# Background modulation units in a two-layer hybrid transformer block: from three engines to VectorE, TensorE and layer 1

## The chip, the cores and the metric

The kernel runs on one core of a Trainium2 chip, as one program. The core has TensorE (PE in the profile; PEld is its weight load), VectorE (DVE), ScalarE (ACT) and GpSimd (POOL); SyncE (SP) issues most DMA transfers. Each engine works through its own queue in order. The metric is device time in microseconds (us) from one launch.

## The reference

Two residual layers run over 512 tokens (`x`) of width 2048, with 256 context tokens beside them. Layer 0 mixes a pooling branch with latent attention, layer 1 a bidirectional mLSTM with windowed attention. What the change touches is the modulation ahead of and behind each layer:

```python
sc = silu(c); scc = silu(c_ctx)                       # two vectors of 2048
for i in range(2):
    shift, scale, gate       = split(sc  @ ada_w[i] + ada_b[i], 3)
    shift_c, scale_c, gate_c = split(scc @ ada_w[i] + ada_b[i], 3)
    h  = rmsnorm(x,  norm_w[i]) * (1 + scale)   + shift
    hc = rmsnorm(xc, norm_w[i]) * (1 + scale_c) + shift_c
    y, yc = mix_i(h, hc)
    x  = x  + gate   * y
    xc = xc + gate_c * yc          # layer 0 only
return rmsnorm(x, final_norm)
```

`ada_w[i]` is a 2048 x 6144 fp32 matrix: two thin vector-matrix products for each layer, of which most of the cost is reading the matrix. The context's gate of layer 1 is not needed.

## The kernel before

**Matmuls.** Activations lie with channels on partitions, as 16 chunks of 128 channels by tokens. Each large fp32 product is made of three fp32r matmuls, of high and low halves of weight and activation. `load_w` (line 111) loads 512 KB of weights by SP's queue into one of three buffers `wraw`, and `split` (line 107) makes the halves: `wh` by a cast on ScalarE (L108), `wl` by a subtraction on VectorE (L109), four buffers each. One such load feeds a quarter of a group: 4 chunks of the contraction by 256 output channels. `tmode` (L289 for the tokens, `px`, 512 columns; L291 for the context, `pc`, 256 columns) and `kmode` (L302) issue the matmuls.

**Modulation units.** The 12,288 modulation columns are cut into 24 units of 512 columns: 0 to 7 shift and scale of layer 0, 8 to 11 its gates, 12 to 19 shift and scale of layer 1, 20 to 23 its gates. A unit reads 4 MB. Units below 20 need two vectors (tokens and context), the four last ones only one. There are two ways to compute a unit:

- `ada_steps` (line 134), used for units 0 to 7 at the start: TensorE multiplies 16 tiles `at` of 128 x 512 fp32 by the columns of `st` (the two vectors, padded to 32 columns), four tiles at a time in four strips of 32 output partitions of one PSUM tile `pa` (L143). VectorE transposes `pa`, and a small matmul `pb` (L150) folds the partial sums.
- `ada_vec_steps` (line 154), used for units 8 to 23 in the background: for each of 16 tiles `at`, VectorE multiplies by the first vector and adds into `acc0` (L162 for the first tile, L164 after that); for two-vector units ScalarE multiplies the same tile by the second vector in place (L167), and GpSimd adds it into `acc1` (L169). Each tile is one step. One more step for each accumulator transposes it (L174) and reduces it (L175). The unit's `pb` matmul (L181) and four small additions (`ada_place`, L131) come 16 steps into the next unit.

`Background` (line 186) strings such units into one sequence of steps, of which other code asks for a number at a time.

**Order of the work.** At the start TensorE's order is written by hand: units 1 to 7 among the first in-projection groups. Behind that the in-projection of layer 0 runs in `in_group` calls for groups 2 to 13 (line 484), four quarters each, with two background steps before and two after each quarter's matmuls: 192 steps are asked for, and units 8 to 17 have 180. Groups 2 and 3 make the query's latent, whose statistics (`cps`, L247) follow; groups 4 to 7 the pooling branch, with `pool_mean` and `pool_mix` between the quarters of 5 and 7; groups 8 to 13 the attention gates. Then comes attention (TensorE's order by hand again), then the out-projection of layer 0, whose function `out0` (line 883) asks for four background steps a quarter: units 18 to 23, 104 steps. Layer 1 begins with `h_chunk` and its in-projection. `mv_group` (line 1164) makes the mLSTM values for three heads, while the gate arithmetic of the mLSTM runs in the pool `gs` on VectorE and ends; `ctx_state` follows each; then group 5. No background runs in layer 1. The layer 1 gates (units 20 to 23) are first used at the very end, in `out_evac`.

Where no order is written by hand, a planner in the compiler lays out each engine's queue from its own estimates of durations, in the program's order as far as operands and buffers are ready. A tile's buffer is given again only when its last reader is done; the queue that asks for it waits. Background tiles have four buffers (`nb`, tag `ada`), shared by all units of the sequence.

Of the kernel before, what the change touches and what calls it, by code (L numbers as in the profile page):

```python
# [8 lines left out]
F32 = mybir.dt.float32  # L9
F32R = mybir.dt.float32r  # L10
AF = mybir.ActivationFunctionType
ALU = mybir.AluOpType
# [4 lines left out]
P = 128  # L17
# [21 lines left out]
def tile_hybrid_dit(ctx: ExitStack, tc: tile.TileContext, ts: dict, out: bass.AP, dbg=None, upto=99):  # L39
# [94 lines left out]
    def ada_steps(u, pp, tp, nb=3, nt=2):  # L134

        pa = pp.tile([P, 512], F32, name=f"pa{u}", tag="pm")
        for q in range(4):
# [13 lines left out]
                ada_place(u, pb, 2)  # L151
            yield

    def ada_vec_steps(u, pp, tp, nb, ttag, tbufs):

        both = u < 20
        acc = [tp.tile([P, 512], F32, name=f"acc{u}_{v}", tag=f"acc{v}", bufs=1) for v in range(2 if both else 1)]
        for kc in range(16):
            at = tp.tile([P, 512], F32, name=f"at{u}_{kc}", tag="ada", bufs=nb)
            DM.dma_start(at, ts["ada"][u, kc // 2][:, (kc % 2) * 512 : (kc % 2) * 512 + 512])  # L160
            if kc == 0:
                V.tensor_scalar(acc[0], at, st[:, kc, 0:1], None, op0=ALU.mult)  # L162
            else:
                V.scalar_tensor_tensor(acc[0], at, st[:, kc, 0:1], acc[0], op0=ALU.mult, op1=ALU.add)  # L164
            if both:
                m = acc[1] if kc == 0 else at
                S.mul(m, at, st[:, kc, 1:2])  # L167
                if kc:
                    G.tensor_tensor(acc[1], acc[1], m, op=ALU.add)  # L169
            yield  # L170
        red = tiny.tile([P, 2, 16], F32, name="red", tag="red", bufs=2)
        for v in range(len(acc)):
            tr = tp.tile([P, 512], F32, name="atr", tag=ttag, bufs=tbufs)
            V.transpose(tr, acc[v])  # L174
            V.tensor_reduce(red[:, v, :], tr.rearrange("p (b r) -> p b r", r=32), axis=AX.X, op=ALU.add)  # L175
            yield

        def finish():
            n = len(acc)
            pb = pp.tile([32, 2, 16], F32, name=f"pb{u}", tag="pm")  # L180
            T.matmul(pb[:, :n, :], fold, red[:, :n, :], start=True, stop=True)  # L181
            ada_place(u, pb, n)

        return finish
# [108 lines left out]
    def kmode(ps, w, kcs, Hs, first, last, share):  # L293

        for i, kc in enumerate(kcs):
            wh, wl = w[i]
            for b, p_ in enumerate(ps):
                Hh, Hl = Hs[kc][0][:, b * P : (b + 1) * P], Hs[kc][1][:, b * P : (b + 1) * P]
                for n, (h_, w_) in enumerate(((Hh, wh), (Hh, wl), (Hl, wh))):
                    s0 = first and i == 0 and n == 0 and b % share == 0  # L300
                    s1 = last and i == len(kcs) - 1 and n == 2
                    T.matmul(p_, h_, w_, start=s0, stop=s1, skip_group_check=True)  # L302
# [96 lines left out]
    with tc.manual_schedule(engines={mybir.EngineType.PE}):  # L399
        ht = Ring(sp, 2)  # L400
# [38 lines left out]
    def ta(name, n=NT):  # L439
        return ap_.tile([P, NP], F32, name=name, tag="ta", bufs=6)[:, :n]  # L440
# [38 lines left out]
    S.copy(kr[:, NX:], pc[:, 0, :])  # L479
    split(kr, KH, KL)  # L480

    bg = Background(range(8, 18), pp, ap_, 4, "ta", 6)

    def in_group(g, between=()):
        px, pc = new_px(2), new_pc()
        for kq in range(4):
            w = load_w(win[g, kq])
            bg.step(2)
            tmode(px, [pc[:, b, :] for b in range(2)], w, range(4 * kq, 4 * kq + 4), HX0, HC0, kq == 0, kq == 3)
            bg.step(2)  # L490
            if kq < len(between):
                between[kq]()
        return px, pc
# [1 line left out]

    ssq = [ap_.tile([P, NT], F32, name="ssqc", tag="ssqc", bufs=1), 0]
    for g in range(2):
        px, pc = in_group(2 + g)
        for b, r in enumerate(c_evac([(px[b], pc[:, b, :]) for b in range(2)], ssq)):
            G.dma_start(cqd[2 * g + b], r)  # L500
    p6 = pp.tile([P, 6], F32, name="cps6", tag="pm")
# [45 lines left out]
        return z  # L547

    for pr in range(2):
        px, pc = in_group(4 + 2 * pr)  # L550
        ds, zs = [], []

        def mean(b):
            ds.append(pool_mean(2 * pr + b, px[b], pc[:, b, :]))

        def mix(b):
            zs.append(pool_mix(2 * pr + b, ds[b]))

        mean(0)
        qx, qc = in_group(5 + 2 * pr, (lambda: mean(1), lambda: mix(0), lambda: None, lambda: mix(1)))  # L560
        for b in range(2):
            t = ta("psg")
            S.activation(t[:, :NX], qx[b], AF.Silu)
            S.activation(t[:, NX:], qc[:, b, :], AF.Silu)
            V.tensor_tensor(t, zs[b], t, op=ALU.mult)
            G.dma_start(zd[2 * pr + b], t)


    for i in range(6):
        px, pc = in_group(8 + i)  # L570
        for b in range(2):
            t = ta("sag")
            S.activation(t[:, :NX], px[b], AF.Silu)
            S.activation(t[:, NX:], pc[:, b, :], AF.Silu)
            G.dma_start(agd[2 * i + b], t)
# [302 lines left out]
    esP.close()  # L878
    esP = ExitStack()
    pp = ppool(esP, "ppO", px=4, pc=2, pm=2)  # L880
    bg = Background(range(18, 24), pp, tz, 4, "ht", 3)

    def out0(g, vs, between=None):
        px = new_px(2) if 0 in vs else None
        pc = new_pc() if 1 in vs else None
        for kq in range(4):
            w = load_w(ts["ev_out"][g, kq])
            if g == 1 and kq < 3:
                zc_load(kq + 1)
            bg.step(4)  # L890
            tmode(px, pc and [pc[:, b, :] for b in range(2)], w, range(4 * kq, 4 * kq + 4), ZX, ZC, kq == 0, kq == 3)
            next(between, None) if between else None
        out0_evac(g, vs, px, pc)

    def stats1(v):

        nb = (4, 2)[v]
        p6 = pp.tile([P, 6], F32, name="ps6b", tag="pm")
        stat_mm(p6[:, :nb], ssq1[v], nb, D)
        rows(rstd_col(p6[:, :nb], nb), nb, pp, ssq1[v])  # L900
# [8 lines left out]
    ehx, ehc, eht = (ExitStack() for _ in range(3))  # L909
    hxp = opool(ehx, "hx", side="right")  # L910
    HX = [(hxp.tile([P, NX], F32R, name=f"hxh{j}"), hxp.tile([P, NX], F32R, name=f"hxl{j}")) for j in range(KC)]
    stats1(0)

    def hx_chunks():
# [7 lines left out]
        out0(g, (1,), hxs)  # L922
    for _ in hxs:
        pass
    bg.finish()
    etz.close()
    ezc.close()

# [232 lines left out]
    eg.close()  # L1161


    def mv_group(h):
        px, pc = new_px(2), new_pc()
        pv = [px[b // 2][:, 256 * (b % 2) : 256 * (b % 2) + 256] for b in range(4)]
        for kq in range(4):
            w = load_w(odw[1 + h, kq])
            kcs = range(4 * kq, 4 * kq + 4)
            kmode(pv, w, kcs, HX, kq == 0, kq == 3, 2)  # L1170
            kmode([pc[:, b, :] for b in range(2)], w, kcs, HC, kq == 0, kq == 3, 2)
        vx_store(h, [p_.rearrange("p (a b) -> p a b", b=256) for p_ in px])
        return vc_store([pc])
# [20 lines left out]
    px, pc = new_px(2), new_pc()  # L1194
    for kq in range(4):
        w = load_w(odw[5, kq])
        tmode(px, [pc[:, b, :] for b in range(2)], w, range(4 * kq, 4 * kq + 4), HX, HC, kq == 0, kq == 3)
    for b in range(2):
        t = cm.tile([P, NX], F32, name="akx", tag="kxt", bufs=2)
        S.copy(t, px[b])  # L1200
        G.dma_start(akd[b][:, :NX], t)
# [630 lines left out]
```

## Time and profile before

| | |
|---|---|
| median of 3 runs | 2345.47 us (2341.54 to 2346.82) |
| profiled execution | 2345.14 us, its span 2343.4 us |
| mean granted TensorE clock | 0.985 |
| TensorE busy | 2238.1 us of the span |
| VectorE, ScalarE, GpSimd busy | 1488.9, 1041.4, 459.0 us |
| background accumulation on VectorE (L164) | 240 instructions, 250.3 us |
| background multiplication on ScalarE (L167) | 180 instructions, 130.0 us |
| background addition on GpSimd (L169) | 180 instructions, 282.7 us |

Rough stages by start in us: start-up and first groups to 180; in-projection groups to 618; attention to 1040; out-projection to 1320; the layer 1 projections, the mLSTM, the windowed attention and the last out-projection to 2343. In a page's rows by line, the two numbers behind the bar are busy time in us and mean duration in ns, and after the second bar stands how long the engine was idle just before them and what ended it. In rows of waits: who waited for whom, us in total, times, longest.

### The profile page before, as it was taken

What the parts mean: (1) busy time and instruction counts of PE and PEld (TensorE: products, weight loads), DVE (VectorE), ACT (ScalarE), POOL (GpSimd) and SP (SyncE); (2) the same over time, 40 slices, a digit from 0 to 9 for tenths busy, and PEclk for the clock granted to TensorE, in tenths of its full rate; (3) what the DMA queues carried; (4) which work ended last, traced back from release to release, by engine and by line L of the source; (5) the groups of instructions that cost most, each with busy time, mean ns of one, the idle gap of its engine ahead of it and who ended that gap; (6) DMA issues with size and microseconds to landing.
All of it is one profiled execution on the core that took longest, in us unless ns stands there. A gap on an engine that the chain in (4) does not pass through costs nothing.

```text
span 2343.4 us, 34744 instructions
## 1 busy us (share of the span) xinstructions
PE 2238.1 (96%) x12920; PEld 1902.8 (81%) x12920; DVE 1488.9 (64%) x2748; ACT 1041.4 (44%) x2054; POOL 459.0 (20%) x393
## 2 busy tenths in 40 slices
PE   5999998999999999999999999999999999999997
PEld 3678887778889999877888898998888877777886
DVE  5578888875476666777767722522555576778435
ACT  4234454443244444554224522222655557666433
POOL 0015565764200000026212200000000010003111
PEclk9999999999999999999999999999999999999998
DMA  9854554563311111255775322123233212113434
GB/s 383 323 197 161 171 185 140 202 205 123 99 57 48 59 52 64 91 186 198 241 248 178 116 95 82 64 73 114 99 99 97 99 62 72 64 55 126 135 113 140
DMA packets 118586, 311.27 MB, mean 133 GB/s; under 512 B 13676, under 2 KB 21356, under 8 KB 118416
## 3 DMA queue, kind: packets, MB, share of 16 engines
q1 hardware_dynamic: 111536, 281.73, 35.9%
q0 software_dynamic: 6880, 27.32, 3.0%
q8 instruction: 101, 1.65, 0.3%
q14 instruction: 69, 0.57, 0.1%
HBM read 279.37 MB, written 29.62 MB: 132 GB/s over the span
## 4 chain that ended last, share of the span: by engine, by line
PE 68%; DVE 9%; issue 4%; DMA 3%; POOL 2%; ACT 2%; DVEq 0%; SPq 0%; ACTq 0%; POOLq 0%
PE px L289 20%; PE px L302 11%; PE pj L619 5%; PE pc L291 5%; PE px L1418 5%; PE s L682 4%; PE pc L302 3%; PE om L725 3%; PE pj L639 2%; POOL acc L169 2%; DMA at<-in_ada_dram 2%; PE s L1418 2%; DVE acc L164 2%; PE po L1337 2%; DVE wl L109 2%
## 5 line engine op out<-in xcount | busy, mean ns | idle before, releaser
L109 DVE TENSOR_TENSOR wl<-wraw,wh 128x512 fp32r<-128x512 f32 (+2 forms) x556 | 431.9, 783 | 420.3 <-ACT wh L108 417.1
L108 ACT CAST wh<-wraw 128x512 fp32r<-128x512 f32 (+2 forms) x556 | 324.5, 589 | 594.7 <-PE pc L291 145.9
L169 POOL TENSOR_TENSOR acc<-acc,at 128x512 f32<-128x512 f32 x180 | 282.7, 1571 | 282.7 <-ACT at L167 272.9
L164 DVE SCALAR_TENSOR_TENSOR acc<-at,st,acc 128x512 f32<-128x512 f32 x240 | 250.3, 1043 | 52.1 <-DMA at<-in_ada_dram 48.3
L167 ACT ACTIVATE at<-at,st 128x512 f32<-128x512 f32 x180 | 130.0, 724 | 180.2 <-DVE acc L164 152.8
L302 PE MATMUL px<-wh,hxh 128*128 128x512 f32 (+2 forms) x512 | 174.4, 341 | 0.1
L302 PE MATMUL px<-wl,hxh 128*128 128x512 f32 (+2 forms) x512 | 173.7, 339 | 0.0
L302 PE MATMUL px<-wh,hxl 128*128 128x512 f32 (+2 forms) x512 | 173.6, 339 | 0.0
L289 PE MATMUL px<-h0h,wl 128*128 128x512 f32 x384 | 155.3, 404 | 11.7 <-DVE wl L109 11.7
L289 PE MATMUL px<-h0h,wh 128*128 128x512 f32 x384 | 156.0, 406 | 1.0 <-ACT wh L108 0.8
L289 PE MATMUL px<-h0l,wh 128*128 128x512 f32 x384 | 153.7, 400 | 0.0
L291 PE MATMUL pc<-h0h,wl 128*128 128x256 f32 x400 | 113.9, 285 | 0.0
L291 PE MATMUL pc<-h0h,wh 128*128 128x256 f32 x400 | 113.7, 284 | 0.0
L291 PE MATMUL pc<-h0l,wh 128*128 128x256 f32 x400 | 113.6, 284 | 0.0
L302 PEld LDWEIGHTS px<-wh,hxh 128*128 128x128 f32 x512 | 96.2, 188 | 12.8 <-ACT sz L1261 1.0
L302 PEld LDWEIGHTS px<-wl,hxh 128*128 128x128 f32 x512 | 96.3, 188 | 11.3
L302 PEld LDWEIGHTS px<-wh,hxl 128*128 128x128 f32 x512 | 96.2, 188 | 11.0
L289 PEld LDWEIGHTS px<-h0h,wl 128*128 128x128 f32 x384 | 73.5, 191 | 32.2 <-DVE wl L109 15.5
L289 PE MATMUL px<-zxh,wl 128*128 128x512 f32 x224 | 88.9, 397 | 3.6 <-DVE wl L109 3.6
L289 PE MATMUL px<-zxh,wh 128*128 128x512 f32 x224 | 89.6, 400 | 2.0 <-ACT wh L108 1.1
L289 PEld LDWEIGHTS px<-h0h,wh 128*128 128x128 f32 x384 | 73.9, 193 | 19.5 <-ACT wh L108 2.5
L289 PE MATMUL px<-hxl,wh 128*128 128x512 f32 x224 | 89.2, 398 | 0.0
(877 smaller groups left out, 6231.7 us busy)
## 6 DMA issues: line engine op xcount, KB each, us to landing
at<-in_ada_dram SPq DMA_DIRECT2D x256, 256.0 KB, 3.1
at<-in_ada_dram SPq DMA_DIRECT2D x64, 512.0 KB, 8.2
wraw<-in_od_in_dram SPq DMA_DIRECT2D x64, 512.0 KB, 3.5
wraw<-in_ev_in_dram SPq DMA_DIRECT2D x56, 512.0 KB, 4.1
wraw<-in_ev_out_dram SPq DMA_DIRECT2D x44, 512.0 KB, 4.5
wraw<-in_od_out_dram SPq DMA_DIRECT2D x36, 512.0 KB, 3.5
wraw<-in_od_oz_dram SPq DMA_DIRECT2D x32, 512.0 KB, 3.5
xt<-in_xT_dram SPq DMA_DIRECT2D x16, 384.0 KB, 7.5
```

Of the source, the lines that this page charges most:

```text
L108: S.copy(h, src)
L109: low.tensor_tensor(l, src, h, op=ALU.subtract)
L164: V.scalar_tensor_tensor(acc[0], at, st[:, kc, 0:1], acc[0], op0=ALU.mult, op1=ALU.add)
L167: S.mul(m, at, st[:, kc, 1:2])
L169: G.tensor_tensor(acc[1], acc[1], m, op=ALU.add)
L289: T.matmul(px[b], w_, Hx[kc][r_], start=s0, stop=s1)
L291: T.matmul(pc[b], w_, Hc[kc][r_], start=s0 and b == 0, stop=s1, skip_group_check=True)
L302: T.matmul(p_, h_, w_, start=s0, stop=s1, skip_group_check=True)
L619: T.matmul(t, w_, r_[:, sl], start=kc == 0 and n == 0, stop=kc == 3 and n == 2)
L682: T.matmul(s[:, c0 - k0 : c1 - k0], l_, r_[:, c0:c1], start=n == 0, stop=n == 4)
L725: T.matmul(o[:, :256], v_[:, 6 - nk + b, :], p_[:, b, :], start=b == 0 and n == 0, stop=b == nk - 1 and n == 2)
L1418: T.matmul(px[b], w_, Hs[kc][r_], start=first and i == 0 and n == 0, stop=last and i == len(kcs) - 1 and n == 2)
```

## The change

Background units no longer use ScalarE (but for the first tile of the second vector) or GpSimd: VectorE accumulates both vectors, so a two-vector step has two accumulations on VectorE. The 16 background units are placed anew:

- units 8 to 13 stay in the in-projection, with two steps before and two after a quarter in groups 2, 3 and 10 to 13, one before a quarter in groups 4 and 6, and none in 5, 7, 8 and 9: 104 steps are asked for, 108 are there, and `bg.finish()` behind group 13 runs the rest;
- units 18 and 19 go to TensorE under groups 8 and 9, by a new function `ada_pe_steps`, which is `ada_steps` with 16 tiles of 256 KB in the four `ada` buffers in place of 8 of 512 KB; one group of four matmuls follows each quarter;
- units 14 to 17, all with two vectors, go to the out-projection of layer 0, three steps a quarter (72 steps), to be finished before layer 1's statistics;
- units 20 to 23, with one vector, go to layer 1: two steps before and three amid each quarter of `mv_group`, two before each quarter of group 5 (68 steps), in a new pool `ada1`, opened when the gate arithmetic's pool is closed.

```diff
+    def ada_pe_steps(u, pp, tp, nb):
+        pa = pp.tile([P, 512], F32, name=f"pa{u}", tag="pm")
+        for q in range(4):
+            at = []
+            for i in range(4):
+                kc = 4 * q + i
+                at.append(tp.tile([P, 512], F32, name=f"at{u}_{kc}", tag="ada", bufs=nb))
+                DM.dma_start(at[i], ts["ada"][u, kc // 2][:, (kc % 2) * 512 : (kc % 2) * 512 + 512])
+            for qd in range(4):
+                T.matmul(pa[32 * qd : 32 * qd + 32, :], st[:, 4 * q + qd, :], at[qd], start=q == 0, stop=q == 3, skip_group_check=True)
+            if q == 3:
+                tr = ta("gat", 512).rearrange("p (b r) -> p b r", r=32)
+                V.transpose(tr.rearrange("p b r -> p (b r)"), pa)
+                yield
+                pb = pp.tile([32, 2, 16], F32, name=f"pb{u}", tag="pm")
+                T.matmul(pb, fold, tr[:, :, 0:2].rearrange("p b v -> p v b"), start=True, stop=True)
+                ada_place(u, pb, 2)
+            yield
...
             if kc == 0:
                 V.tensor_scalar(acc[0], at, st[:, kc, 0:1], None, op0=ALU.mult)
+                if both:
+                    S.mul(acc[1], at, st[:, kc, 1:2])
             else:
-                V.scalar_tensor_tensor(acc[0], at, st[:, kc, 0:1], acc[0], op0=ALU.mult, op1=ALU.add)
-            if both:
-                m = acc[1] if kc == 0 else at
-                S.mul(m, at, st[:, kc, 1:2])
-                if kc:
-                    G.tensor_tensor(acc[1], acc[1], m, op=ALU.add)
+                for v, a in enumerate(acc):
+                    V.scalar_tensor_tensor(a, at, st[:, kc, v : v + 1], a, op0=ALU.mult, op1=ALU.add)
...
-    bg = Background(range(8, 18), pp, ap_, 4, "ta", 6)
+    bg = Background(range(8, 14), pp, ap_, 4, "ta", 6)
-    def in_group(g, between=()):
+    def in_group(g, between=(), steps=(1, 1)):
...
-            bg.step(2)
+            bg.step(steps[0])
             tmode(px, [pc[:, b, :] for b in range(2)], w, range(4 * kq, 4 * kq + 4), HX0, HC0, kq == 0, kq == 3)
-            bg.step(2)
+            bg.step(steps[1])
...
-        px, pc = in_group(2 + g)
+        px, pc = in_group(2 + g, steps=(2, 2))
...
-        px, pc = in_group(4 + 2 * pr)
+        px, pc = in_group(4 + 2 * pr, steps=(1, 0))
...
-        qx, qc = in_group(5 + 2 * pr, (lambda: mean(1), lambda: mix(0), lambda: None, lambda: mix(1)))
+        qx, qc = in_group(5 + 2 * pr, (lambda: mean(1), lambda: mix(0), lambda: None, lambda: mix(1)), (0, 0))
...
-        px, pc = in_group(8 + i)
+        if i < 2:
+            pe = ada_pe_steps(18 + i, pp, ap_, 4)
+            px, pc = in_group(8 + i, (lambda: next(pe), lambda: next(pe), lambda: next(pe), lambda: (next(pe), next(pe))), (0, 0))
+        else:
+            px, pc = in_group(8 + i, steps=(2, 2))
...
-    bg = Background(range(18, 24), pp, tz, 4, "ht", 3)
+    bg = Background(range(14, 18), pp, tz, 4, "ht", 3)
...
-            bg.step(4)
+            bg.step(3)
...
+    bg.finish()
     stats1(0)
...
-    bg.finish()
     etz.close()
...
+    ea = ExitStack()
+    bg = Background(range(20, 24), pp, opool(ea, "ada1"), 4, "atr", 1)
     def mv_group(h):
...
+            bg.step(2)
             kmode(pv, w, kcs, HX, kq == 0, kq == 3, 2)
+            bg.step(3)
             kmode([pc[:, b, :] for b in range(2)], w, kcs, HC, kq == 0, kq == 3, 2)
...
+        bg.step(2)
         tmode(px, [pc[:, b, :] for b in range(2)], w, range(4 * kq, 4 * kq + 4), HX, HC, kq == 0, kq == 3)
+    bg.finish()
+    ea.close()
```

## Prediction

> **What bounds the kernel now.** I read the page first, then busy time by stage, then TensorE's own waits, then the shapes on each engine inside the stage that the change empties.
>
> ```profile
> span 2343.4 us, 34744 instructions
> PE 2238.1 (96%) x12920; PEld 1902.8 (81%) x12920; DVE 1488.9 (64%) x2748; ACT 1041.4 (44%) x2054; POOL 459.0 (20%) x393
> PE   5999998999999999999999999999999999999997
> DVE  5578888875476666777767722522555576778435
> POOL 0015565764200000026212200000000010003111
> PE 68%; DVE 9%; issue 4%; DMA 3%; POOL 2%; ACT 2%; DVEq 0%; SPq 0%; ACTq 0%; POOLq 0%
> ```
>
> TensorE is busy in 96% of the span, so what can be won is the rest, wherever background work makes it. The stages, in order (columns after the stretch: its length, then busy time and count per engine, granted clock, DMA share, GB/s):
>
> ```profile
> 180.00:240.00 60.00, 60.00 (x347) 52.55 (x346) 52.30 (x54) 29.45 (x46) 35.99 (x25) 1.00 0.50 163
> 240.00:520.00 280.00, 257.45 (x1386) 218.87 (x1386) 239.02 (x265) 129.58 (x213) 179.12 (x127) 0.96 0.53 179
> 520.00:618.00 98.00, 98.00 (x563) 85.25 (x562) 48.13 (x62) 29.54 (x51) 26.86 (x21) 1.00 0.37 121
> 1040.00:1240.00 200.00, 195.25 (x1065) 166.35 (x1064) 148.03 (x199) 61.92 (x100) 75.16 (x64) 1.00 0.70 232
> 1350.00:1454.00 104.00, 104.00 (x677) 95.15 (x676) 22.27 (x49) 26.34 (x50) 3.99 (x11) 1.00 0.28 92
> 1454.00:1605.00 151.00, 150.63 (x1178) 142.90 (x1177) 58.07 (x168) 36.52 (x65) 2.41 (x8) 1.00 0.20 68
> ```
>
> From 240 to 520 us, in the in-projection, TensorE stands still for 280 − 257.45 = 22.5 us, and a mean granted clock of 0.96 takes another 0.04 × 280 = 11.2 us: 33.7 us. This is the purse. VectorE is busy for 239 of the 280 us. In layer 1 (1454 to 1605) TensorE has no hole and VectorE is at 38%. Who ends the holes (TensorE's waits, 200 to 600 us):
>
> ```profile
> PE px L289 <- DVE wl L109: 11.7, 11, 1.9
> PE ppx L545 <- ACT wpoolh L108: 4.3, 1, 4.3
> PE cps L247 <- DVE ssqc L454: 3.2, 1, 3.2
> PE pb L181 <- ACT pz L546: 2.4, 1, 2.4
> PE px L289 <- ACT wh L108: 0.8, 1, 0.8
> ```
>
> The sum is 22.4 us; 12.5 of it waits for split weights. Why they are late, from VectorE's, GpSimd's and ScalarE's groups of that stretch and all engines' waits there:
>
> ```profile
> L164 DVE SCALAR_TENSOR_TENSOR acc<-at,st,acc 128x512 f32<-128x512 f32 x135 | 154.7, 1146 | 27.5 <-DMA at<-in_ada_dram 25.5
> L109 DVE TENSOR_TENSOR wl<-wraw,wh 128x512 fp32r<-128x512 f32 x86 | 102.6, 1207 | 42.9 <-ACT wh L108 42.7
> L174 DVE STREAM_TRANSPOSE atr<-acc 128x512 f32<-128x512 f32 x20 | 13.4, 692 | 1.3 <-POOL acc L169 1.2
> L175 DVE TENSOR_REDUCE red<-atr 128x16 f32<-128x512 f32 x20 | 12.9, 668 | 0.1
> L162 DVE TENSOR_SCALAR acc<-at,st 128x512 f32<-128x512 f32 x9 | 4.2, 468 | 0.0
> L169 POOL TENSOR_TENSOR acc<-acc,at 128x512 f32<-128x512 f32 x136 | 214.6, 1578 | 91.9 <-ACT at L167 84.3
> ACT at L167 <- DVE acc L164: 121.9, 73, 3.6
> SPq L160 <- POOL acc L169: 206.0, 129, 4.5
> ...
> L164 DVE SCALAR_TENSOR_TENSOR acc<-at,st,acc x240: 734/752/1868, 149.5 to 1240.0; 128x512 f32<-128x512 f32 x120
> L109 DVE TENSOR_TENSOR wl<-wraw,wh x556: 404/691/2068, 38.5 to 2324.8; 128x512 fp32r<-128x512 f32 x163, 128x256 fp32r<-128x256 f32 x18, 128x272 fp32r<-128x272 f32 x5
> ```
>
> The last two rows are minimum, median and longest over the whole span. The accumulation is 752 ns at the median but 1146 on average here, the weight subtraction 691 against 1207, and here GpSimd adds for 215 us. I read that as GpSimd slowing VectorE. The chain VectorE, ScalarE, GpSimd also holds each `at` buffer: ScalarE waits 121.9 us for it in order, ahead of weight casts, and SP's queue 206 us, ahead of weight loads.
>
> **The change, part by part.** *(a) VectorE's load.* With no GpSimd adds I take the medians. A two-vector unit costs VectorE 0.47 + 15 × 2 × 0.752 + 2 × (0.692 + 0.668) = 25.8 us in 18 steps, so four steps 5.7 us; with two weight subtractions of 0.691 a quarter of a group needs 7.1 us. TensorE's price for that quarter comes from the chain in order of time (start, length):
>
> ```profile
> 1395.35 5.60 PE px L289 x24
> 1400.94 2.80 PE pc L302 x24
> ```
>
> 24 matmuls of 512 columns and 24 of 256: 8.4 us. So VectorE is covered where four steps stay (groups 2, 3, 10 to 13), and nearly free in 4 to 9. If the means held (1.146 and 1.207) it would need 10.7 us, 2.3 too many in each of 24 quarters: 55 us, the far bound, which the median speaks against.
>
> *(b) The holes.* Split weights, 12.5 us: ScalarE's multiply and GpSimd's add vanish from all three in-order queues; I leave 1.5 us. The two at the pool mix, 6.7 us: steps go from groups 5 and 7; I leave 2.0. The statistics (`cps`), 3.2 us, is a VectorE chain behind group 3, which keeps its steps; I leave 2.2. Returned: 16.7 of 22.4. The clock loss follows its holes: 11.2 × 16.7 / 22.4 = 8.4. Together −25.1; bounds 0 and −33.7.
>
> The stretch 240 to 280 us, which holds that one `cps` wait of 3.2 us:
>
> ```profile
> 240.00:280.00 40.00, 36.82 (x196) 31.99 (x196) 32.40 (x42) 17.72 (x28) 24.93 (x19) 0.91 0.54 181
> ```
>
> A clock of 0.91 there is 3.6 us. [...]
>
> *(c) Units 18 and 19 on TensorE.* The start-up runs eight such units:
>
> ```profile
> L143 PE MATMUL pa<-at,st 128*32 128x512 f32 x256 | 34.5, 635 | 0.9 <-PE pb L150 0.9
> ```
>
> 34.5 / 8 = 4.3 us each, four column strips at once; two units +8.6. There an order by hand keeps the four together; here the planner places them. If all 32 went alone, at two records of 635 ns each, it is at most 40.6. I take 8.6: they are issued together behind a quarter's matmuls. [...]
>
> *(d) The tail.* The groups call 104 of 108 steps; `finish` runs four more behind group 13: 4 × 0.752 + 2.7 = 5.7 us of VectorE. From 520 to 618 it was busy for 48 of 98 us, so part hides. +1.0 (0 to 5.7).
>
> *(e) The out-projection.* Its waits of TensorE:
>
> ```profile
> PE px L289 <- DVE wl L109: 3.6, 3, 1.9
> PE px L289 <- ACT wh L108: 1.1, 1, 1.1
> ```
>
> Four two-vector units at three steps: 4.3 + 1.4 = 5.7 us under a quarter of 8.4, which hides them in groups 1 to 5; in group 6, without context, the quarter is 5.6, a wash. GpSimd's `acc` adds leave. −2.0 (−4.7 to +3).
>
> *(f) Layer 1.* 68 steps of about 0.75 us, 51 us of VectorE on 58 in 151: hidden. The queue on which it could show is SP's: the new pool may take space that the gate arithmetic still uses, and an `at` load that waits for it would hold the weight loads behind it. The arithmetic ends here:
>
> ```profile
> L1147 DVE TENSOR_TENSOR mcol<-mcol,beta x1: 193/193/193, 1487.3 to 1487.3; 128x32 f32<-128x32 f32 x1
> ```
>
> That is 33 us after 1454. Three raw weight buffers of 8.4 us each cover 25 of it; 8 would show at worst, and the full 33 without the cover. I take +0.5 (0 to 8), since the loads stay short of the end of their cover if the planner sees the wait. The state products (`ctx_state`), which wait for VectorE in order too, are in that 0.5. The small matmuls `pb` only change place.
>
> Sum: −25.1 + 8.6 + 1.0 − 2.0 + 0.5 = −17.0. The profiled execution took 2345.14 us (span 2343.4), 0.3 under the median of the runs shown: 2345.1 − 17.0 = 2328.
>
> **The rivals.** *The holes stay by half.* VectorE is still at 7.1 / 8.4 = 85% where four steps remain, as in 240 to 520 now (239 / 280), and an in-order queue that full can be late wherever a statistics or pool step falls in. Half the purse of (b), −12.6, with no gain in (e): −12.6 + 8.6 + 1.0 + 0.5 = −2.5: 2343. Against it: 180 to 240 us has the same four steps and a full TensorE.
>
> *TensorE waits for its own units; slower.* Place: the eight groups of four in 8 and 9. The ring has four `at` buffers, exactly one group deep, so the next four loads start only when TensorE has read the last, and TensorE's queue is in order: every in-projection matmul stands behind the waiting one. One load lands in:
>
> ```profile
> at<-in_ada_dram SPq DMA_DIRECT2D x256, 256.0 KB, 3.1
> ```
>
> Four and a weight load are 1.5 MB, 8.4 us at the stage's 179 GB/s, just the quarter. If each came 3 us late, with the purse's half us of clock (11.2 / 22.4) for each us of hole behind it, it is 8 × 4.5 = 36: 2364. It decides from 17 / 8 = 2.1 us per group on, 1.4 late and 0.7 of clock. Against it: 179 GB/s is demand, not a limit; the out-projection draws 232.
>
> *All holes close.* −33.7 + 8.6 − 4.7 = −29.8: 2315. For it: three queues lose their cross waits at once; against it, the `cps` chain is still there.
>
> **How the numbers follow.** Forecast 0.66, holes by half 0.15, slower 0.12, all closed 0.07. Less than 0.2% (4.7 us) can't be told from no change here. The forecast's own spread, 2317 to 2339, and the closed case lie below 2340.8; of the half case some 0.04 does, 0.10 is no change, 0.01 slower; the forecast gives 0.01 to no change. Faster 0.66 − 0.01 + 0.07 + 0.04 = 0.76, same 0.11, slower 0.13. The range runs from the closed case to just past the half case, 2315 to 2344, and leaves out the slower rival and a little below.
>
> **What would show it.** Right: no GpSimd additions before 600 us; VectorE's accumulation near 0.75 us and the weight subtraction near 0.69 on average there; TensorE's holes in the in-projection at 6 us or less and its clock at 0.99; new `pa` matmuls of some 9 us in total; layer 1 without a hole. Wrong: accumulations still above 1 us; waits of `pa` on `at`; a new hole near 600 us or in layer 1.

## The result and the profile after

The changed kernel takes 2319.8 us (median of 4 runs, 2318.4 to 2322.6); the kernel before, run on the same chip, 2343.5 us (median of 4, 2336.6 to 2346.8). The ratio is 0.9902, with a 95% interval from 0.9887 to 0.9917. The profiled execution took 2320.82 us, 24.3 less than the one before; its span is 24.4 us shorter. The forecast was 2328 us, 17.0 less. The sign is right; that the size comes near is in part luck, since two of the stages below miss their forecast by 10 us and more, in opposite directions.

From the page of the kernel after: the span, each engine's busy time, and TensorE's busy tenths in 40 slices of the span.

```profile
span 2319.0 us, 34267 instructions
PE 2232.1 (96%) x12984; PEld 1897.7 (82%) x12984; DVE 1414.7 (61%) x2860; ACT 922.0 (40%) x1872; POOL 177.0 (8%) x213
PE   5999999999899999999999999899999989999997
```

GpSimd lost 282 us of work (459.0 us before). VectorE does more instructions (2860, before 2748) in less time (1414.7 us, before 1488.9). TensorE has three slices at 8, where the kernel before had one: near 600 us, near 1480 and near 1880.

Where the time was won and lost is read from three places that both programs pass: the last gate group of the in-projection is evacuated (`sag`, the end of the column "first and last start"), the last query projection of layer 1 (`mqt`), and the first `akx`, behind the last layer 1 projection. First the kernel before, then after (minimum, median, longest; first and last start).

```profile
L573 ACT ACTIVATE sag<-px x12: 585/592/598, 449.0 to 619.4; 128x512 f32<-128x512 f32 x12
L951 ACT ACTIVATE mqt<-px x4: 575/597/602, 1327.7 to 1350.9; 128x512 f32<-128x512 f32 x4
L1200 ACT COPY akx<-px x2: 578/582/586, 1603.6 to 1604.9; 128x512 f32<-128x512 f32 x2
```

```profile
L595 ACT ACTIVATE sag<-px x12: 588/594/603, 411.0 to 587.9; 128x512 f32<-128x512 f32 x12
L973 ACT ACTIVATE mqt<-px x4: 576/598/602, 1291.0 to 1314.2; 128x512 f32<-128x512 f32 x4
L1231 ACT COPY akx<-px x2: 578/582/587, 1577.9 to 1579.3; 128x512 f32<-128x512 f32 x2
```

| stage | before, us | after, us | change | forecast, and from which steps |
|---|---|---|---|---|
| start to the last `sag` | 619.4 | 587.9 | −31.5 | −16.5, (b) and (c) |
| to the last `mqt` | 731.5 | 726.3 | −5.2 | −1.0, (d) and (e) |
| to the first `akx` | 252.7 | 263.7 | +11.0 | +0.5, (f) |
| to the end of the span | 739.8 | 741.1 | +1.3 | 0 |
| sum | 2343.4 | 2319.0 | −24.4 | −17.0 |

The busy times by stretch of the kernel after (its length, busy time and count per engine, granted clock, DMA share, GB/s):

```profile
180.00:520.00 340.00, 339.90 (x1955) 288.68 (x1955) 183.45 (x293) 78.10 (x140) 17.06 (x27) 1.00 0.48 158
588.00:590.00 2.00, 0.09 (x2) 0.00 (x0) 1.82 (x6) 1.05 (x4) 0.93 (x2) 1.00 0.00 0
591.15:596.90 5.75, 5.75 (x28) 5.69 (x29) 2.37 (x9) 0.00 (x0) 0.00 (x0) 0.50 1.00 354
1420.00:1575.00 155.00, 147.38 (x1135) 139.56 (x1134) 105.52 (x247) 32.94 (x59) 1.87 (x7) 0.98 0.53 174
1507.30:1511.60 4.30, 4.30 (x20) 4.30 (x21) 3.29 (x7) 0.73 (x2) 0.00 (x0) 0.50 0.91 281
```

From 180 to 520 us TensorE has no hole left and its full clock. Behind the last gate group stands a new hole of 3.1 us, which ends at 591.15, and behind it TensorE works for 5.75 us at a clock of 0.50: another 2.9 us. In layer 1, where TensorE was full before (150.63 of 151 us, clock 1.00), 7.6 us are idle, and behind the longest hole TensorE works for 4.3 us at half clock, another 2.2 us: 9.8 of the loss of 11. TensorE's longest waits between 180 and 1610 us name the two places:

```profile
PE pc L1215 <- ACT wvh L108: 6.6, 2, 6.2
PE pj L641 <- DVE vl L109: 3.2, 1, 3.2
PE pb L199 <- DVE red L193: 3.1, 1, 3.1
PE ps6b L265 <- DVE ssq L885: 3.0, 1, 3.0
```

The second was there before (3.3 us, for `knl`). The third is the tail of the background work. The first is in layer 1: TensorE waits for the cast of the state product `wv`. VectorE's timeline there (start, length, in brackets the idle time before it):

```profile
1497.00 2.33 DVE L187 SCALAR_TENSOR_TENSOR acc<-at,st,acc 128x512 f32<-128x512 f32 x3
1502.42 2.33 DVE L187 SCALAR_TENSOR_TENSOR acc<-at,st,acc 128x512 f32<-128x512 f32 x3 [3.09 <-DMA at<-in_ada_dram]
1504.67 0.68 DVE L109 TENSOR_TENSOR wl<-wraw,wh 128x512 fp32r<-128x512 f32 x1
1505.28 0.74 DVE L187 SCALAR_TENSOR_TENSOR acc<-at,st,acc 128x512 f32<-128x512 f32 x1
1505.94 0.61 DVE L1207 TENSOR_SCALAR wv<-vcx,wcol 128x258 f32<-128x258 f32 x2
```

ScalarE's copy `vcx`, the operand of the product, began at 1498.79 and took 0.59 us, so `wv` could have begun near 1499.4. It begins at 1505.94. In front of it in VectorE's in-order queue stand four accumulations and a weight subtraction, and the first of them waits 3.09 us for a load. VectorE's waits for such loads between 1420 and 1575 us (in all, times, longest), and the loads' median time to landing over the whole span and from 1455 to 1510 us:

```profile
DVE acc L187 <- DMA at<-in_ada_dram: 16.1, 12, 3.1
at<-in_ada_dram SPq DMA_DIRECT2D x256, 256.0 KB, 3.4
at<-in_ada_dram SPq DMA_DIRECT2D x41, 256.0 KB, 3.9
```

The rows that the forecast named for the steps themselves:

```profile
L187 DVE SCALAR_TENSOR_TENSOR acc<-at,st,acc 128x512 f32<-128x512 f32 x360 | 253.2, 755 | 23.6 <-DMA at<-in_ada_dram 22.5
L109 DVE TENSOR_TENSOR wl<-wraw,wh 128x512 fp32r<-128x512 f32 (+2 forms) x556 | 371.2, 673 | 491.6 <-ACT wh L108 472.0
L164 PE MATMUL pa<-at,st 128*32 128x512 f32 x64 | 8.5, 605 | 0.0
```

The accumulation takes 755 ns on average, and the two units on TensorE 8.5 us (those 64 records lie between 300 and 470 us) with no wait in front of them.

### The profile page after: what moved, and what is told of

Its sections match the earlier page's. It is cut to its first block, busy times and chain, and to the rows that moved or that the text cites. A ratio compares the mean times of both kernels' runs of the same rounds, so it can differ in the third digit from the quotient of the medians.

```text
span 2319.0 us, 34267 instructions
## 1 busy us (share of the span) xinstructions
PE 2232.1 (96%) x12984; PEld 1897.7 (82%) x12984; DVE 1414.7 (61%) x2860; ACT 922.0 (40%) x1872; POOL 177.0 (8%) x213
## 4 chain that ended last, share of the span: by engine, by line
PE 62%; DVE 6%; DMA 2%; issue 2%; ACT 1%; POOL 0%; DVEq 0%; SPq 0%; ACTq 0%; POOLq 0%
PE px L307 17%; PE px L320 10%; PE pj L641 5%; PE px L1449 5%; PE s L704 4%; PE pc L309 3%; PE om L747 3%; PE pc L320 2%; PE s L1449 2%; PE pj L661 2%; PE po L1368 2%; PE tp L729 2%; DMA at<-in_ada_dram 1%; PE wpt L1611 1%; DVE wl L109 1%
## 5 line engine op out<-in xcount | busy, mean ns | idle before, releaser
L109 DVE TENSOR_TENSOR wl<-wraw,wh 128x512 fp32r<-128x512 f32 (+2 forms) x556 | 371.2, 673 | 491.6 <-ACT wh L108 472.0
L307 PE MATMUL px<-hxh,wh 128*128 128x512 f32 x224 | 89.5, 400 | 0.0
L307 PE MATMUL px<-zxl,wh 128*128 128x512 f32 x224 | 89.3, 399 | 0.0
L307 PE MATMUL px<-hxh,wl 128*128 128x512 f32 x224 | 89.2, 398 | 0.0
```

The source lines that it names most:

```text
L109: low.tensor_tensor(l, src, h, op=ALU.subtract)
L307: T.matmul(px[b], w_, Hx[kc][r_], start=s0, stop=s1)
```

## The experiments

Three questions: what earns the 40 us of the in-projection (31.5 us of the first stage, and the 8.5 that the units on TensorE take there), what the new placing costs, and why layer 1 lost 11 us. Ratios are against the kernel before, run on the same chip.

**The arithmetic alone.** The kernel before with one edit; units, stages and steps stay where they were.

```diff
@@ before: ada_vec_steps
             if kc == 0:
                 V.tensor_scalar(acc[0], at, st[:, kc, 0:1], None, op0=ALU.mult)
+                if both:
+                    S.mul(acc[1], at, st[:, kc, 1:2])
             else:
-                V.scalar_tensor_tensor(acc[0], at, st[:, kc, 0:1], acc[0], op0=ALU.mult, op1=ALU.add)
-            if both:
-                m = acc[1] if kc == 0 else at
-                S.mul(m, at, st[:, kc, 1:2])
-                if kc:
-                    G.tensor_tensor(acc[1], acc[1], m, op=ALU.add)
+                for v, a in enumerate(acc):
+                    V.scalar_tensor_tensor(a, at, st[:, kc, v : v + 1], a, op0=ALU.mult, op1=ALU.add)
```

> The kernel before with one thing changed: both vectors are accumulated by VectorE; units and steps stay where they were (units 8 to 17 in the in-projection, four steps in each quarter; 18 to 23 in the out-projection). If it is the GpSimd additions that made VectorE late: its accumulation falls from 1.146 us to about 0.76 on average in the in-projection, a quarter needs 7.1 of its 8.4 us, the 22.4 us of holes shrink below 6, and with no units on TensorE and none in layer 1 the time is 2305 to 2318. If it is the number of steps that made VectorE late: 180 steps of 1.43 us keep it as busy as before, the holes stay above 15 us, and the time is 2333 to 2345.

Measured: 2295.8 us (2295.5 to 2297.1), ratio 0.9793 (0.9774 to 0.9812): 24 us faster than the changed kernel, and 9 us below the range that was expected. Busy times of its in-projection, and its accumulation between 180 and 480 us (minimum, median, longest):

```profile
240.00:320.00 80.00, 80.00 (x464) 69.94 (x465) 76.01 (x127) 22.10 (x39) 4.24 (x8) 1.00 0.64 204
240.00:480.00 240.00, 240.00 (x1386) 209.70 (x1387) 221.65 (x361) 60.70 (x109) 11.00 (x20) 1.00 0.65 206
L167 DVE SCALAR_TENSOR_TENSOR acc<-at,st,acc x257: 735/746/1198, 182.5 to 469.3; 128x512 f32<-128x512 f32 x129
```

All ten units stay under the in-projection, VectorE is busy for up to 76.01 of 80 us, 95%, and TensorE has no hole from 240 to 480 us. The move of the second vector to VectorE earns everything. The units did not have to go anywhere.

**The placing alone.** The changed kernel with the old arithmetic put back (the edit above the other way round).

> The changed kernel with one thing undone: the second vector again goes through ScalarE and GpSimd; the placing of units and steps is the changed one. If the GpSimd additions made VectorE late: holes of 8 us or more come back in groups 2, 3 and 10 to 13 and some in the out-projection, where four two-vector units now run; 2328 to 2345. If the placing earned the gain: holes in the in-projection below 4 us and a time within 5 us of 2320.

Measured: 2362.0 us (2359.2 to 2363.8), ratio 1.0077 (1.0053 to 1.0101): slower than before, and slower than either of the two cases expected. VectorE's and GpSimd's groups from 180 to 520 us:

```profile
L184 DVE SCALAR_TENSOR_TENSOR acc<-at,st,acc 128x512 f32<-128x512 f32 x51 | 58.9, 1155 | 11.6 <-DMA at<-in_ada_dram 10.8
L189 POOL TENSOR_TENSOR acc<-acc,at 128x512 f32<-128x512 f32 x51 | 79.4, 1556 | 40.1 <-ACT at L187 37.5
```

With fewer units there, the accumulation beside GpSimd's additions is as slow as it was (1155 ns, before 1146). The holes in layer 1 come with the placing: `pc` waits 8.0 us for `wvh`. The arithmetic put back here does not reach them, as the units there have one vector.

**GpSimd's additions without their chain.** The 1146 ns before could have come from the chain between three engines and not from the engines' company. So the changed kernel gets two additions on GpSimd per step of units 8 to 13, on constants, into a tile that nobody reads.

```diff
+        idle = None
+        if u < 14:
+            idle = tp.tile([P, 224], F32, name=f"idle{u}", tag="idle", bufs=1)
...
+            if both and idle is not None and kc:
+                for _ in range(2):
+                    G.tensor_tensor(idle, vec[:, 0:224], con[:, 0:224], op=ALU.add)
```

> The changed kernel with added work on GpSimd that nobody waits for: with each step of units 8 to 13, two additions of constants, 128 x 224, into a spare tile. No buffer and no queue that the matmuls need hangs on it, so it adds contention alone. If GpSimd slows VectorE by running beside it: VectorE's accumulation is above 1.0 us on average where GpSimd is busy, the weight subtraction above 1.0, holes of 8 us or more appear in the in-projection, and the time is 2328 to 2350. If it was the chain of queues (at buffers held by GpSimd, ScalarE waiting ahead of weight casts): the accumulation stays at 0.76, no hole appears, 2316 to 2324.

Measured: one run, 2395.5 us. VectorE's accumulation and weight subtraction and GpSimd's additions from 240 to 310 us:

```profile
L190 DVE SCALAR_TENSOR_TENSOR acc<-at,st,acc x40: 1142/1152/1158, 239.1 to 297.7; 128x512 f32<-128x512 f32 x40
L109 DVE TENSOR_TENSOR wl<-wraw,wh 128x512 fp32r<-128x512 f32 x15 | 15.8, 1081 | 0.0
L193 POOL TENSOR_TENSOR idle<-vec,con 128x224 f32<-128x224 f32 x65 | 63.0, 969 | 5.0
```

Nothing waits for these additions, and still each of the 40 accumulations takes 1142 to 1158 ns in place of some 750, and the weight subtraction of the same shape 1081 in place of 691. So GpSimd's company alone makes these two longer, the accumulation by 0.40 us each time. That size belongs to these small additions: in the kernel before, between 180 and 520 us, where GpSimd made the real ones of 128x512, the same accumulation took 737 ns at least, 845 at the median and up to 1868, so some paid nothing (one of 0.74 us, at 255.52 us, lies within additions that ran from 253.75 to 260.15) and others over 1 us. And these runs do not separate how much of the 22.4 us of holes the longer instructions made and how much the chain of queues, since the first experiment takes both away. The run's time is no price of that, though: the edit also put work in front of another's in GpSimd's queue.

```profile
DVE kr L341 <- POOL rt L340: 32.6, 1, 32.6
```

A product of the rope, `rt`, stood behind the constant additions, and VectorE with everything behind it waited 32.6 us for it. TensorE's longest wait for weights, 37.2 us up to 230.33, ends just behind it (228.08).

**The tail, and the place of the steps in layer 1.** In the changed kernel groups 4 and 6 get two steps a quarter in place of one, so that nothing is left behind group 13; and the value projections of layer 1 take their steps in the first three quarters, away from the state products.

```diff
-        px, pc = in_group(4 + 2 * pr, steps=(1, 0))
+        px, pc = in_group(4 + 2 * pr, steps=(1, 1))
...
-            bg.step(2)
+            n = (7, 7, 6, 0)[kq]
+            bg.step(n // 2)
             kmode(pv, w, kcs, HX, kq == 0, kq == 3, 2)
-            bg.step(3)
+            bg.step(n - n // 2)
```

> The changed kernel with its two new holes taken out. Groups 4 and 6 get one step more in each quarter, so all 108 steps are done before group 13 ends; in the value groups of layer 1 the 20 steps of a group are spread 7, 7, 6, 0 over the quarters, so none stands ahead of the state products. If the hole of 6.2 us in layer 1 comes from accumulations queued ahead of the state's products on VectorE, and the 3.1 us hole near 588 us from the tail: both go with the half clock behind them, 5 to 6 and 8 to 10 us: 2303 to 2308. If layer 1's hole comes from VectorE's load as such, it moves to another quarter, and the time is 2312 to 2316.

Measured: 2316.9 us (2313.0 to 2317.4), ratio 0.9878 (0.9858 to 0.9899). Busy times around the end of the in-projection, TensorE's wait between 1410 and 1620 us, and VectorE's between 1455 and 1510:

```profile
585.00:600.00 15.00, 14.87 (x110) 13.91 (x110) 5.44 (x15) 4.73 (x13) 1.11 (x2) 1.00 0.50 176
PE pc L1216 <- ACT wvh L108: 8.4, 2, 5.8
DVE acc L187 <- DMA at<-in_ada_dram: 11.4, 7, 4.2
```

The hole of the tail is gone. From the last `sag` (588.6 us here) to the first evacuation of the out-projection (1036.6) it takes 448.0 us, 4.4 less than in the changed kernel (587.9 to 1040.3). Layer 1 keeps its loss: the number of steps asked for in the last quarter isn't what puts the accumulations ahead of the products, and that theory falls. Accumulations wait 11.4 us for loads just there.

**Later loads or too few buffers.** In layer 1, six buffers for `at` in place of four.

```diff
-    bg = Background(range(20, 24), pp, opool(ea, "ada1"), 4, "atr", 1)
+    bg = Background(range(20, 24), pp, opool(ea, "ada1"), 6, "atr", 1)
```

> The changed kernel with six buffers in place of four for the background tiles of layer 1. VectorE waited there for loads that land 3.6 us after their issue, with the state's products queued behind the waiting accumulation. If late loads make the 6.2 us hole of layer 1: with two loads more in flight VectorE's waits on them nearly go, the hole falls to 3 us or less, and the time is 2311 to 2316. If the number of accumulations queued ahead of the products makes it: the hole stays at 5 to 7 us, 2317 to 2322.

Measured: 2316.2 us (2313.4 to 2318.9), ratio 0.9876 (0.9862 to 0.9891). Against the changed kernel (2319.8) that is too little for the times to tell apart; the profile tells more:

```profile
PE pc L1215 <- ACT wvh L108: 4.2, 3, 3.8
DVE acc L187 <- DMA at<-in_ada_dram: 4.2, 6, 1.9
```

TensorE's wait falls from 6.6 to 4.2 us, as VectorE's waits for loads fall (from 16.1 to 4.2 us between 1420 and 1575). The stretch from the last `mqt` to `akx` is 260.9 us in place of 263.7. Earlier loads help, and don't suffice: 4.2 us lies between the two cases expected.

**Without the loads.** In the changed kernel units 20 to 23 load only the first of their 16 tiles, and all 16 accumulations read it, so the computation of four of layer 1's gates is left out while VectorE's work stays.

```diff
-            at = tp.tile([P, 512], F32, name=f"at{u}_{kc}", tag="ada", bufs=nb)
-            DM.dma_start(at, ts["ada"][u, kc // 2][:, (kc % 2) * 512 : (kc % 2) * 512 + 512])
+            if u < 20 or kc == 0:
+                at = tp.tile([P, 512], F32, name=f"at{u}_{kc}", tag="ada", bufs=nb)
+                DM.dma_start(at, ts["ada"][u, kc // 2][:, (kc % 2) * 512 : (kc % 2) * 512 + 512])
```

> The changed kernel, but in units 20 to 23 only the first of 16 tiles is loaded and all 16 accumulations read it (so the gates of layer 1 are left out, the arithmetic's time is kept): VectorE has the same work in layer 1 and never waits for a load. If late loads ahead of the state's products make the hole of layer 1: holes there sum to below 1.5 us and the time is 2308 to 2313. If the accumulations themselves, queued ahead, make it: 4 us or more of holes stay, 2316 to 2321.

Measured: 2312.7 us (2304.0 to 2315.7), ratio 0.9856 (0.9829 to 0.9883). Busy times of layer 1's projections and TensorE's wait there:

```profile
1420.00:1575.00 155.00, 153.81 (x1195) 145.04 (x1195) 109.35 (x257) 37.80 (x67) 2.74 (x9) 1.00 0.22 76
PE pc L1216 <- ACT wvh L108: 1.0, 2, 0.9
```

VectorE is busy for 109.35 of 155 us, more than in the changed kernel, and the hole shrinks from 6.6 to 1.0 us; the clock stays full; the stretch takes 254.8 us, 8.9 less. So the loss in layer 1 is not VectorE's load but the loads that the accumulations ahead of the state's products wait for. At the place of the timeline above the queue still has accumulations, a weight subtraction and an accumulation ahead of `wv`, yet `wv` begins 1.2 us behind the end of `vcx` (1502.29, after 1500.49 + 0.59), where it was 6.6. Elsewhere the planner can have ordered the work otherwise with the loads gone, so the 8.9 us may hold some of that too.

**Fewer units in layer 1.** Units 20 and 21 go to the out-projection.

```diff
-    bg = Background(range(14, 18), pp, tz, 4, "ht", 3)
+    bg = Background([*range(14, 18), 20, 21], pp, tz, 4, "ht", 3)
...
-    bg = Background(range(20, 24), pp, opool(ea, "ada1"), 4, "atr", 1)
+    bg = Background(range(22, 24), pp, opool(ea, "ada1"), 4, "atr", 1)
```

> The changed kernel with two units (20 and 21) moved back from layer 1 to the out-projection of layer 0, whose quarters then take 106 of 120 steps; layer 1 keeps two units, 34 steps asked for in its first two value groups. If the hole of layer 1 comes from accumulations that pile up because the pool is free only when the gate arithmetic ends: half as many leave the hole behind the second value group, the one of 6.2 us, gone or under 2 us; 2309 to 2315. If any accumulation among the products is enough: the hole stays behind one of the first two groups at 4 us or more, and the time is within 3 us of 2320.

Measured: 2341.8 us (2337.9 to 2346.6), ratio 0.9992 (0.9981 to 1.0002). The edit missed its question: six units are 106 steps, the groups ahead of the statistics call 84, and `finish` ran the other 22 in one lump.

```profile
1255.55 0.26 PE L199 MATMUL pb<-red,con 128*32 128x16 f32 x2 [3.90 <-DVE red L193]
1275.14 0.55 PE L309 MATMUL pc<-zch,wh 128*128 128x256 f32 x1 [14.05 <-DVE x L876]
1254.00:1282.00 28.00, 11.28 (x53) 10.71 (x54) 21.23 (x44) 13.50 (x22) 8.15 (x7) 0.51 0.15 47
```

An evacuation stood behind the lump on VectorE, and TensorE waited 14.0 us for it, up to 1275.14. The 28 us at a clock of 0.51 hold that wait: the clock (1.00 from 1235 to 1254) had fallen at about 1254, in the wait of 3.9 us ahead of it, and most of the low clock fell on a TensorE that stood still. It says nothing on layer 1, and shows step (d) at full size: what `finish` leaves for the end falls on TensorE.

**The units on TensorE.** The kernel with the mended tail, and units 18 and 19 on VectorE under the in-projection as well.

```diff
-    bg = Background(range(8, 14), pp, ap_, 4, "ta", 6)
+    bg = Background([*range(8, 14), 18, 19], pp, ap_, 4, "ta", 6)
...
-        if i < 2:
-            pe = ada_pe_steps(18 + i, pp, ap_, 4)
-            px, pc = in_group(8 + i, (lambda: next(pe), lambda: next(pe), lambda: next(pe), lambda: (next(pe), next(pe))), (0, 0))
-        else:
-            px, pc = in_group(8 + i, steps=(2, 2))
+        px, pc = in_group(8 + i, steps=(2, 2) if i < 5 else (3, 2))
```

> The version with both new holes' steps moved (2316.9 us), with units 18 and 19 back on VectorE: eight units in the in-projection, two steps before and two after a quarter in groups 8 and 9 as well. If a unit on TensorE costs just its 4.3 us and VectorE has room: 8.5 us less, 2306 to 2310. If VectorE's steps make holes there: 2312 to 2317.

Measured: 2306.0 us (2303.7 to 2307.5), ratio 0.9839 (0.9824 to 0.9855), 10.9 us less than with the units on TensorE (2316.9). The row of the matmuls gives 8.5 of it; the runs of each kernel spread over some 4 us, which doesn't separate 10.9 from 8.5. From 180 to 520 us TensorE is as full as with the units on it:

```profile
180.00:520.00 340.00, 339.89 (x1957) 296.97 (x1956) 245.73 (x395) 84.00 (x148) 18.19 (x29) 1.00 0.52 171
```

So these matmuls were bought at their full price, and what they took off VectorE was worth nothing. That price looks higher than the row. Around the first burst of the changed kernel (start, length):

```profile
381.67 0.28 PE L309 MATMUL pc<-h0h,wl 128*128 128x256 f32 x1
381.88 1.07 PE L164 MATMUL pa<-at,st 128*32 128x512 f32 x8
382.87 0.50 PE L307 MATMUL px<-h0h,wh 128*128 128x512 f32 x1
383.21 0.28 PE L309 MATMUL pc<-h0h,wh 128*128 128x256 f32 x1
```

From one `pc` to the next it takes 1.54 us; without a burst it is 0.35 (381.32 to 381.67). That is 1.19 us for each of eight bursts, 9.5 in all. And the last `sag` starts at 576.8 us without the units and at 588.6 with them, 11.8 us apart; what lies between 9.5 and 11.8 I have not located.

**A version that beats both.** The first experiment's kernel, with more of GpSimd's two-input work off that engine too: first the low halves of the query latent, then also the sums of squares of the out-projection and layer 1's low halves.

```diff
-    c_norm(raw, rq, cq, V_QN, tf, pp, G)
+    c_norm(raw, rq, cq, V_QN, tf, pp)
@@ only in the second of the two
-                    (G if j < KC - 1 else V).tensor_tensor(ssq1[v], ssq1[v], sq[:, PARTS[v]], op=ALU.add)
+                    V.tensor_tensor(ssq1[v], ssq1[v], sq[:, PARTS[v]], op=ALU.add)
...
-            h_chunk(j, x1[j], ssq1, 12, 1, *((HX[j][i], None) for i in range(2)), Ring(tz, 3), (0,), G if j % 2 else V)
+            h_chunk(j, x1[j], ssq1, 12, 1, *((HX[j][i], None) for i in range(2)), Ring(tz, 3), (0,), V)
```

> As the kernel before with both vectors on VectorE (2295.8 us), and only the low halves of the query latent moved from GpSimd to VectorE. If contention makes the 3.3 us hole at the start of attention: it falls below 1.5 us, 2290 to 2295. If the four subtractions are better kept off VectorE: the hole grows, 2296 to 2300.

> The kernel before with both vectors on VectorE, units and steps where they were (2295.8 us), and with the other GpSimd arithmetic from attention's start to layer 1 moved to VectorE too: the low halves of the query latent, the sums of squares of the out-projection, and half of the low halves of layer 1's activations. If GpSimd beside VectorE costs time wherever TensorE waits for VectorE: the 3.3 us hole at the start of attention and those of the out-projection's end shrink, 2285 to 2293. If there GpSimd's help is worth more than its contention: 2296 to 2305.

Measured: 2293.4 us (2292.5 to 2297.8), ratio 0.9783 (0.9768 to 0.9798), and 2290.7 us (2288.1 to 2292.0), ratio 0.9765 (0.9749 to 0.9782). TensorE's waits at two places in the first experiment's kernel, and then in the second of these:

```profile
PE pj L617 <- DVE knl L109: 3.3, 1, 3.3
PE ps6b L245 <- DVE ssq L861: 1.9, 1, 1.9
```

```profile
PE pj L617 <- DVE wl L109: 1.3, 1, 1.3
PE pj L617 <- DVE knl L109: 0.4, 1, 0.4
PE ps6b L245 <- DVE ssq L861: 0.5, 1, 0.5
```

3.3 us at the start of the attention became 1.7, and 1.9 at the statistics 0.5. Whether GpSimd's slowing of VectorE made these holes, or GpSimd's own slowness (its subtractions for the latent took 2291 ns each), is not separated. The second version is the fastest of all, 29 us under the changed kernel; against the first experiment (2295.8) the intervals of both versions overlap.

## Why the prediction was right or wrong

**(a) VectorE's load: right.** The medians of the trace before were the prices after: 755 ns for 752, 673 for 691. The far bound of 55 us rested on the means beside GpSimd, and the constant additions show that GpSimd's company is enough to lengthen these instructions (the accumulation to 1152 ns at the median, the subtraction to 1081 on average).

**(b) The holes: right in kind, 8.6 us too small, and drawn too narrow.** The step kept 1.5 us for the split weights, 2.0 for the pool mix, 2.2 for `cps` and the clock that goes with them. All of it came back: from 180 to 520 us TensorE is busy for 339.90 of 340 us at clock 1.00. The pool mix and the statistics were not late by the length of their own chains: the first experiment closes these holes too, with the full load of steps in those groups. Whether GpSimd's slowing of VectorE or the chain of queues made each of them late stays open. And the purse began at 240 us. The row of the kernel before for 140 to 180 us, and the same of after:

```profile
140.00:180.00 40.00, 36.49 (x216) 31.60 (x215) 35.33 (x55) 21.46 (x35) 13.00 (x9) 0.96 0.38 125
```

```profile
140.00:180.00 40.00, 39.27 (x243) 33.55 (x243) 33.75 (x63) 17.86 (x30) 0.00 (x0) 1.00 0.35 112
```

Another 2.8 us of hole and 0.04 × 40 = 1.6 of clock were to be had there. With the purse that is 33.7 + 4.4 = 38.1; less (c)'s 8.5 it leaves 29.6 of the 31.5 us of the first stage. The last 1.9, or up to 5.2 if (c) cost the 11.8 below, I have not located.

**(c) The units on TensorE: right in kind, priced a little low.** 8.6 was forecast; the row gives 8.5, the starts around the bursts 9.5, the times without the units 10.9 and the first stage 11.8. Eight bursts stand among the in-projection's matmuls, and the planner kept each together: a burst costs 8.5 / 8 = 1.06 us by the row and 1.19 from start to start.

**(d) The tail: the right place, undersized.** +1.0 was taken of 0 to 5.7 us of VectorE's work. The hole is 3.1 us, and 2.9 us of clock followed it: 6.0. The step priced the hole and forgot the clock, which in (b) it had counted for every hole. Mending it gains 4.4 us of the stage, so its net price is 4.4 to 6.0.

**(e) The out-projection: right in sign, too small with its neighbour.** (d) and (e) together gave −5.2 where −1.0 was forecast; with (d) at 4.4 to 6.0, (e) and what lies with it gave some −10 to −11. Of the −5.2, −2.4 lies ahead of the first evacuation of the out-projection (1074.2 us before, 1040.3 after), with (d) in it, and −2.8 behind. The 4.7 us of waits that the step quoted are all gone, and part of the rest is clock; I did not divide it further.

**(f) Layer 1: wrong.** +0.5 (0 to 8) was forecast, +11.0 came. The step watched SP's queue and the space of the pool. It put the state products "in that 0.5" without pricing them, though it named their mechanism: VectorE's queue is in order. "51 us of VectorE on 58 in 151: hidden" is an average over the stage. In 1497 to 1506 us the products stood behind accumulations that wait for a load. The run without loads takes 8.9 of the 11 back. Two of the prediction's own signs of being wrong appeared with (d) and (f): a new hole near 600 us, and one in layer 1. Why the planner puts those accumulations first is open: that it reckons with loads landing sooner than they do is only argued. These loads land in 3.9 us at the median there, over the whole span in 3.4, and before the change in 3.1.

**The rivals.** *All holes close* (0.07) is what happened in the in-projection, and its total of 2315 was near only because layer 1 took 11 us back. *The holes stay by half* fell: it argued that VectorE at 85% would be late, and at 95% it isn't. *TensorE waits for its own units* fell: the row of `pa` has 0.0 us of idle before it, and taking the units off TensorE gained what their matmuls cost. The likeliest case was right in the direction and in most of its mechanism, but near in its total by luck: some 19 us more than forecast in the first two stages stood against 12 us lost behind them. And I asked of the placing only what each move costs, never what the kernel would be without it: the arithmetic alone was 24 us better.

## What to carry to other kernels

Before work is moved off a busy VectorE, look whether its instructions have a minimum far under their mean while GpSimd adds, as the accumulation of the kernel before has (734 ns at least, 1043 on average over the span); taking that work back can leave VectorE with less to do, not more (1460.1 us busy in the first experiment, 1488.9 before). Then try the change of engine alone, ahead of any new placing: a busy engine that was still ahead of its consumer cost nothing here (VectorE busy for 76.01 of 80 us, TensorE without a hole), and moving its work did (10.9 us for two units on TensorE). And where background work goes into a new stage, look for the products on the path that share its in-order queue, and for the loads in front of them; that VectorE was busy for 38% of the stage before hid neither.

## What the runs showed of the hardware

- GpSimd's additions of 128x224 on constants lengthened VectorE's 128x512 accumulation from about 750 ns to 1142 to 1158, nearly the same 0.40 us for each of 40. With the real additions of 128x512, in the kernel before from 180 to 520 us, it was a spread: 737 to 1868 ns, 845 at the median.
- VectorE was busy for 76.01 of 80 us without one late weight for TensorE (the first experiment, 240 to 320 us: TensorE busy for 80.00).
- The clock fell at short holes: one of 3.1 us (to 591.15) was followed by 5.75 us of work at a clock of 0.50, and the fall came about 1.9 us into it, as the row from 588 to 590 us still has 1.00 and the clock from 590.00 to 591.15 is 0.52. In the kernel before, a wait of 1.88 us that ended at 434.06 was followed by a clock of 0.50 from 435.05 to 438.47.
